# Hybrid conformer block on one core: the first head's far statistics by ScalarE's queue, and the output merges' first transfers earlier in the program

## The chip, the cores and the metric

The kernel runs on one core of one Trainium2 chip. The metric is the device time of one execution in microseconds (us). The core's engines are TensorE (PE, matmuls), VectorE (DVE), ScalarE (ACT), GpSimd (POOL) and SyncE (SP), which here only issues transfers (DMAs). Each engine runs its own instructions in order and waits for the others on semaphores. SyncE and ScalarE each have a queue on which they start DMAs; in the profile these appear as SPq and ACTq.

## What is computed

One block on 1024 tokens of width 1024, in float32: a norm, one wide projection, a gated depthwise convolution branch, an attention branch with 16 heads, a gated merge of the two, an output projection, and a gated feed-forward network. For this change the attention and the merge matter:

```python
DILATION_GROUPS = ((128, 1), (512, 4), (2048, 16))
...
    m = jnp.max(scores, axis=-1, keepdims=True)
    p = jnp.exp(scores - m)
    den = jnp.sum(p, axis=-1)
    o = jnp.einsum('nbhqk,nbkhd->nbqhd', p, vc) / jnp.swapaxes(den, 2, 3)[..., None]
    lse = jnp.swapaxes(m[..., 0] + jnp.log(den), 2, 3)
...
        mix = jax.nn.softmax(jnp.stack(lses), axis=0)
        o = jnp.einsum('gbsh,gbshd->bshd', mix, jnp.stack(outs))
        o = o.astype(x.dtype).reshape(B, S, ATTN_DIM)
        y_b = o @ w_attn_out[l].astype(o.dtype)

        g = jax.nn.sigmoid(gate_logits + gate_b[l].astype(gate_logits.dtype))
        g_a, g_b = jnp.split(g, 2, axis=-1)
        x = x + (g_a * y_a + g_b * y_b) @ w_out[l].astype(x.dtype)

        h = rms_norm(x, norm2_g[l])
```

Each query attends within three groups of keys (near ones, every fourth, every sixteenth), and the three softmaxes are mixed by the sums of their exponentials.

## The kernel before

**Products in three parts.** A float32 product is made of three TensorE passes: each operand is split into a high part (`hi`, rounded by ScalarE, L99) and a low part (`lo`, the rest, subtracted by VectorE, L100). The lines L131 to L133 are the three passes `hi*hi`, `hi*lo`, `lo*hi` of one step over 128 rows.

**The attention stage.** It is a loop over slots, eight for each of the 16 heads, four for each half of the queries. On ScalarE, VectorE, TensorE and GpSimd the order is written out by hand: it is the order in which the loop makes the instructions. SyncE's order is the scheduler's. In slot `at` the scores of the current unit are made (`score`, L1056 and L1057, the far group L1092), VectorE takes minima (`least`, L1060), and ScalarE takes exponentials with row sums (`powers`, L1101). Twelve slots later (`BACK = 12`) the unit is transposed by TensorE into a tile `pp` (`flip`, L1153), split into `ph` and `pl` (L1174, L1175), and two slots behind that multiplied with the values (`weigh`, L1191 and L1192). Between these, pieces of another matmul (the gate logits, later the convolution's output) fill TensorE (`fill`).

**The statistics.** For the second half of the queries a near part and a far part have minima and sums of their own, `own[h]`, in different layouts. Each part needs those of the other, `other[h]`. `near_to_far` sends the near part by four small transfers from SBUF to SBUF (L1118); `far_out` writes the far part to DRAM (`dstat`, L1121), and `far_to_near` reads it back in the other layout (L1125), five slots after the far scores (`READ = 5`). Then `compare` (L1129, L1130) and `combine` (L1135 to L1138) make the shares, and GpSimd multiplies the exponentials by them (`times`, L1104: four far products, then four near ones). The transposes of the far unit and of the second half wait for these. For the first head, whose far scores are made in slot 4, `far_to_near` stands in slot 9, `compare` in slot 13 and `combine` in slot 14; its far transposes stand in slot 16. For the other heads `compare` and `combine` stand one slot earlier each in relation to the head.

`tc.issue_after(x)` adds an edge of order behind `x` for what the block makes on the engine of `x`, and no wait across engines.

**The output merges.** When the heads are done, the attention output `do_` is read back from DRAM in pairs of rows (`o_fetch`: a raw part into a buffer `raw`, and a second part into the tile `oT`), added and split (`o_step`, L1228, L1224, L1221). Four `raw` buffers serve these and the weights (`stage`, L104; `wpiece`). Then `merge(c, w, half)` runs 16 times: three transfers (L1341 to L1343) bring two gate logits and the convolution branch into a tile `gg` (three buffers), ScalarE takes two sigmoids (L1346, L1347), VectorE multiplies (L1348), TensorE makes `yb` in one of four PSUM banks (24 matmuls), VectorE multiplies `yb` by its gate (L1355) and adds (L1356), and the sum is split into `mT` (L1358, L1359). The first four merges use the first half of the tokens, the next four the second half of the same weights. The row `gb2`, the second norm's factors spread over all partitions, is loaded ahead of the merges (L1336) and first read in the output projection (L1461).

Of the kernel before, what the change touches and what calls it, by code (L numbers as in the profile page):

```python
# [21 lines left out]
P = 128  # L22
# [47 lines left out]
def block_kernel(ctx: ExitStack, tc: tile.TileContext, x, xT, x0, g2, pack, mask,  # L70
# [957 lines left out]
    if True:  # L1028
# [94 lines left out]
        def far_to_near(h):  # L1123
            with tc.issue_after(queued[0].ins):
                sp.dma_start(other[h][:, 0], dstat[h % 2].rearrange("(i a) r s -> (a r) i s", i=4))  # L1125
# [83 lines left out]

        def o_fetch(half, k):  # L1210
            cs = slice(half * 512, half * 512 + 512)
            part = lambda i: do_[k : k + 2, i, :, cs].rearrange("k p t -> p k t")
            raw = stage(part(0), f"o_{half}{k}").rearrange("p (a b) -> p a b", a=2)
            hi, lo = (oT[i][half][:, k : k + 2, :] for i in range(2))
            fetch(lo, part(1))
            return raw, hi, lo
# [23 lines left out]
        with tc.manual_schedule(engines={ENG.Activation, ENG.DVE, ENG.PE, ENG.Pool}):  # L1240
# [3 lines left out]
            for at in range(len(slots) + BACK + 1):  # L1244
# [20 lines left out]
                for n, soon in enumerate(COPIES):  # L1265
                    if at == 0 and soon < 0 or cur is not None and (at - soon) % 8 == 0 and at - soon < len(slots):
                        by_residue((at - soon) // 8 if at else 0, n)
                flips = []
# [12 lines left out]
                for ago, ready in ((BACK - 3, combine), (BACK - 4, compare)):  # L1281
                    then = at - ago - (at < BACK + 4)
                    if 0 <= then < len(slots) and slots[then][1:] == (1, 0):
                        ready(slots[then][0])
# [16 lines left out]
                if at == len(slots) + BACK - 1:  # L1301
                    ao_first = [wpiece(w_ao[0], "ao0")]
# [22 lines left out]
    if True:  # L1325
        for a in range(2):
            oT[a].append(hb2_tile([P, KT, 512], F32R, f"hb{a}1", f"oT{a}1"))
        with tc.issue_after(settled_o[3].ins):
            ao_first += [wpiece(w_ao[c], f"ao{c}") for c in range(1, 4)]
        for k in range(0, KT, 2):  # L1330
            later = [o_fetch(1, k)]
            for _ in range(3):
                o_step(later)
        mT = hb_tiles(hb1, "mT")
        gb2 = p3.tile([P, D], F32, name="gb2")
        sp.dma_start(gb2, bass.AP(tensor=g2.tensor, offset=g2.offset, ap=[[0, P], [1, D]]))  # L1336
        def merge(c, w, half, between=None):
            cs = slice(half * 512, half * 512 + 512)
            gg = p3.tile([P, 3, 512], F32, tag="e", bufs=3, name=f"gg_{c}_{half}")
            ga, gb, ya = gg[:, 0], gg[:, 1], gg[:, 2]  # L1340
            sp.dma_start(ga, dgate[c][:, cs])  # L1341
            sp.dma_start(gb, dgate[8 + c][:, cs])
            sp.dma_start(ya, dya[c][:, cs])  # L1343
# [4 lines left out]
            dve.tensor_tensor(out=ya, in0=ya, in1=ga, op=ALU.mult)  # L1348
            yp = bank_ps(f"yb_{c}_{half}")
# [113 lines left out]

        for tt in range(8):
# [474 lines left out]
```

## Time and profile before

| What | us |
|---|---|
| three runs, median (lowest to highest) | 1667.54 (1666.99 to 1669.13) |
| the profiled execution | 1668.18 |
| its span in the trace | 1666.0 |
| TensorE busy | 1658.0 |
| VectorE busy | 1244.6 |
| ScalarE busy | 919.6 |
| GpSimd busy | 406.5 |

The granted TensorE clock was 1.00 throughout. Times in the trace are counted from the span's start. In a timeline row the first number is the start, the second the duration, both in us; then come engine, line of the kernel, operation, output<-input, partitions x elements, and how many instructions the row stands for. Brackets at the end give the idle time before the row and what ended it. In the view of waits the three numbers are the total in us, how often, and the longest. "DMA to landing" is the time from the issue of a transfer to its completion. Matmul durations are modelled and overlap, so the distance from start to start tells what one costs.

### The profile page before, as it was taken

The page shows a single profiled execution, that of the slowest core. Times are in us where ns is not written, and L with a number is a line of the kernel's source. Part 1 is how long each engine was busy: PE and PEld are TensorE (multiplying, and loading weights), DVE is VectorE, ACT ScalarE, POOL GpSimd, SP SyncE. Part 2 cuts the span into 40 slices and gives each one's busy share as a digit, 9 for nine tenths or more (in the row PEclk, how much of TensorE's full clock was granted, in tenths as well). Part 3 has the DMA queues.
Part 4 walks back from the last instruction along what each step waited for, and adds up shares of the span by engine and source line. Part 5 has one row for each costly group of instructions (what it writes and reads, how often), then busy time and mean ns, then how long its engine had stood idle before and what let it go on. Part 6 is the DMA issues. An engine that isn't in the chain of part 4 may idle for free.

```text
span 1666.0 us, 23008 instructions
## 1 busy us (share of the span) xinstructions
PE 1658.0 (100%) x7867; PEld 1384.3 (83%) x7867; DVE 1244.6 (75%) x1996; ACT 919.6 (55%) x1748; POOL 406.5 (24%) x450
## 2 busy tenths in 40 slices
PE   9999999999999999999999999999999999999999
PEld 7888888888888888888878888888888888888887
DVE  6999887879784568777567645878777777789863
ACT  5565555776665578777655434554444554544431
POOL 0023344877752355555310000000000000000000
PEclk9999999999999999999999999999999999999999
DMA  9111235344345879888587685422222222598851
GB/s 358 31 59 51 101 114 202 101 125 166 107 134 195 295 243 302 278 252 241 163 292 265 223 306 187 167 78 87 89 85 80 76 89 89 170 379 299 283 170 51
DMA packets 182341, 290.84 MB, mean 175 GB/s; under 512 B 31952, under 2 KB 89936, under 8 KB 181712
## 3 DMA queue, kind: packets, MB, share of 16 engines
q1 hardware_dynamic: 180928, 285.05, 51.2%
q10 hardware_dynamic: 1296, 4.33, 0.7%
q8 instruction: 62, 1.02, 0.2%
q14 instruction: 55, 0.45, 0.1%
HBM read 209.50 MB, written 79.76 MB: 174 GB/s over the span
## 4 chain that ended last, share of the span: by engine, by line
PE 96%; DMA 1%; DVE 1%; issue 1%; ACT 1%; POOL 0%; SPq 0%; POOLq 0%; DVEq 0%; ACTq 0%
PE dx L1745 7%; PE xz L156 6%; PE xz L158 6%; PE xz L157 6%; PE dy L1745 5%; PE qkv L150 5%; PE qkv L148 5%; PE qkv L149 5%; PE gx L158 3%; PE gx L156 3%; PE gx L157 3%; PE y L156 2%; PE y L158 2%; PE y L157 2%; PE pp L1153 2%; PE wo L150 2%
## 5 line engine op out<-in xcount | busy, mean ns | idle before, releaser
L572 POOL TENSOR_TENSOR codd<-codd,cpart 128x513 f32<-128x513 f32 x112 | 147.8, 1322 | 132.8 <-DVE lo_s L100 56.1
L148 PE MATMUL qkv<-qkv_hi,hT 128*128 128x512 f32 x384 | 152.7, 398 | 0.0
L150 PE MATMUL qkv<-qkv_hi,hT 128*128 128x512 f32 x384 | 150.3, 391 | 0.0
L149 PE MATMUL qkv<-qkv_lo,hT 128*128 128x512 f32 x384 | 149.9, 390 | 0.0
L1648 DVE SCALAR_TENSOR_TENSOR u<-u,pk 128x1023 f32<-128x1023 f32 x88 | 112.2, 1277 | 1.2 <-ACT u L1646 0.9
L621 DVE SCALAR_TENSOR_TENSOR conv<-csum,both,conv 128x512 f32<-128x512 f32 x120 | 90.2, 752 | 2.3 <-ACT conv L653 0.2
L621 DVE SCALAR_TENSOR_TENSOR conv<-apad,pk,conv 128x512 f32<-128x512 f32 x120 | 90.1, 751 | 1.6
L150 PEld LDWEIGHTS qkv<-qkv_hi,hT 128*128 128x128 f32 x384 | 72.1, 188 | 15.6
L149 PEld LDWEIGHTS qkv<-qkv_lo,hT 128*128 128x128 f32 x384 | 72.3, 188 | 14.6
L148 PEld LDWEIGHTS qkv<-qkv_hi,hT 128*128 128x128 f32 x384 | 72.2, 188 | 14.3
L100 DVE TENSOR_TENSOR lo_uv<-raw_uv,hi_uv 128x1024 fp32r<-128x1024 f32 x20 | 24.5, 1226 | 79.3 <-ACT hi_uv L99 79.3
L1175 DVE TENSOR_TENSOR pl<-pp,ph 128x512 fp32r<-128x512 f32 (+1 forms) x95 | 58.8, 619 | 30.4 <-ACT ph L1174 29.3
L586 ACT ACTIVATE cpart<-apad,pk 128x513 f32<-128x513 f32 x112 | 76.6, 744 | 2.1 <-POOL codd L572 2.0
L1060 DVE CUSTOM_DVE_ANT_0 p<-s,m 128x512 f32<-128x512 f32 (+1 forms) x120 | 59.1, 503 | 21.7 <-POOL p L1104 16.2
L156 PE MATMUL xz<-h2left,hi_uv 128*128 128x512 f32 x176 | 68.6, 390 | 0.0
L156 PE MATMUL xz<-blk_t,hi_s3g 128*128 128x512 f32 x176 | 68.5, 389 | 0.0
L158 PE MATMUL xz<-h2left,lo_uv 128*128 128x512 f32 x176 | 68.5, 389 | 0.0
L158 PE MATMUL xz<-blk_t,lo_s3g 128*128 128x512 f32 x176 | 68.5, 389 | 0.0
L157 PE MATMUL xz<-h2left,hi_uv 128*128 128x512 f32 x176 | 68.5, 389 | 0.0
L157 PE MATMUL xz<-blk_t,hi_s3g 128*128 128x512 f32 x176 | 68.5, 389 | 0.0
L1174 ACT ACTIVATE ph<-pp 128x512 fp32r<-128x512 f32 (+1 forms) x95 | 51.2, 539 | 28.4 <-PE pp L1153 27.6
L124 POOL TENSOR_TENSOR rs<-ss,mhalf 128x8 f32<-128x8 f32 x32 | 53.6, 1677 | 36.3 <-DVE ss L123 34.2
(479 smaller groups left out, 5185.2 us busy)
## 6 DMA issues: line engine op xcount, KB each, us to landing
wr<-w_down SPq DMA_DIRECT2D x45, 512.0 KB, 6.1
kk<-dk SPq DMA_DIRECT2D x32, 512.0 KB, 6.1
gr<-dff SPq DMA_DIRECT2D x62, 256.0 KB, 5.6
raw_qkv<-w_qkv SPq DMA_DIRECT2D x24, 512.0 KB, 4.6
raw_g<-w_ch SPq DMA_DIRECT2D x23, 512.0 KB, 3.7
dff<-u SPq DMA_DIRECT2D x22, 512.0 KB, 2.6
raw_uv<-w_up SPq DMA_DIRECT2D x21, 512.0 KB, 3.6
raw_ug<-w_up SPq DMA_DIRECT2D x20, 512.0 KB, 3.7
```

Source lines behind the costliest of these rows:

```text
L148: pe.matmul(ps, ah, hi[:, k % 2, :], start=(k == 0), stop=False)
L149: pe.matmul(ps, ah, lo[:, k % 2, :], start=False, stop=False)
L150: end = pe.matmul(ps, al, hi[:, k % 2, :], start=False, stop=(k == KT - 1))
L156: pe.matmul(o, wh[:, k, :], bh[:, k, :], start=(start and k == 0), stop=False, skip_group_check=not start)
L157: pe.matmul(o, wh[:, k, :], bl[:, k, :], start=False, stop=False, skip_group_check=not start)
L158: end = pe.matmul(o, wl[:, k, :], bh[:, k, :], start=False, stop=(k == 3), skip_group_check=not start)
L572: r = pool.tensor_tensor(out=out, in0=in0, in1=in1, op=op)
L586: act.activation(part, zo[:, i : i + 513], AF.Copy, scale=taps[:, c, 2 * i + 1 : 2 * i + 2])
L621: dve.scalar_tensor_tensor(out=out_, in0=src[:, i : i + 512], scalar=w, in1=out_, op0=ALU.mult, op1=ALU.add)
L1060: dve.tensor_tensor_reduce(out=pt, in0=s, in1=m, scale=-1.0, scalar=3e38, op0=ALU.add, op1=ALU.min, accum_out=nm)
L1648: dve.scalar_tensor_tensor(out=acc[:, d:], in0=src[:, : T - d], scalar=w(2 - d), in1=acc[:, d:], op0=ALU.mult, op1=ALU.add)
L1745: pe.matmul(banks[n][:, cols], a[:, c], b[:, d], start=(start and i == 0 and m == 0), stop=(stop and i == nf - 1 and m == 2), skip_group_c ...
```

## The change

Two places are changed.

In the attention stage the first head's `far_to_near` is issued by ScalarE instead of SyncE. The first head's `compare` stays in slot 13 but stands ahead of that slot's `flip`, and its `combine` moves from slot 14 to slot 13, behind `weigh` and `result`. The other heads keep their slots.

Ahead of the merges the raw parts of the first two pairs of the second half (`o_raw`) and the second weight piece (`ao1`) are loaded in the loop's last slot but one, in the order ao0, ao1, o part 0, o part 2. The transfers, sigmoids and first product of the first merge (`gate_pair(0, 0)`) stand ahead of the last `o_fetch`. The `gb2` row is loaded behind the last merge's transfers.

```diff
         def far_to_near(h):
             with tc.issue_after(queued[0].ins):
-                sp.dma_start(other[h][:, 0], dstat[h % 2].rearrange("(i a) r s -> (a r) i s", i=4))
+                (sp if h else act).dma_start(other[h][:, 0], dstat[h % 2].rearrange("(i a) r s -> (a r) i s", i=4))
...
+        o_raws = {}
+
+        def o_part(half, k, i):
+            return do_[k : k + 2, i, :, half * 512 : half * 512 + 512].rearrange("k p t -> p k t")
+
+        def o_raw(half, k):
+            return stage(o_part(half, k, 0), f"o_{half}{k}").rearrange("p (a b) -> p a b", a=2)
+
         def o_fetch(half, k):
-            cs = slice(half * 512, half * 512 + 512)
-            part = lambda i: do_[k : k + 2, i, :, cs].rearrange("k p t -> p k t")
-            raw = stage(part(0), f"o_{half}{k}").rearrange("p (a b) -> p a b", a=2)
+            raw = o_raws.pop((half, k)) if (half, k) in o_raws else o_raw(half, k)
             hi, lo = (oT[i][half][:, k : k + 2, :] for i in range(2))
-            fetch(lo, part(1))
+            fetch(lo, o_part(half, k, 1))
             return raw, hi, lo
...
+                if at == BACK + 1:
+                    compare(0)
                 flips = []
...
                 for ago, ready in ((BACK - 3, combine), (BACK - 4, compare)):
-                    then = at - ago - (at < BACK + 4)
-                    if 0 <= then < len(slots) and slots[then][1:] == (1, 0):
-                        ready(slots[then][0])
+                    if BACK <= at - ago < len(slots) and slots[at - ago][1:] == (1, 0):
+                        ready(slots[at - ago][0])
+                if at == BACK + 1:
+                    combine(0)
...
                 if at == len(slots) + BACK - 1:
-                    ao_first = [wpiece(w_ao[0], "ao0")]
+                    ao_raws = [stage(w_ao[c], f"ao{c}") for c in range(2)]
+                    for k in (0, 2):
+                        o_raws[1, k] = o_raw(1, k)
+                    ao_first = [wpiece(w_ao[0], "ao0", ao_raws[0])]
...
         with tc.issue_after(settled_o[3].ins):
-            ao_first += [wpiece(w_ao[c], f"ao{c}") for c in range(1, 4)]
+            ao_first += [wpiece(w_ao[c], f"ao{c}", ao_raws[1] if c == 1 else None) for c in range(1, 4)]
+        gated = {}
+
+        def gate_pair(c, half):
+            cs = slice(half * 512, half * 512 + 512)
+            gg = p3.tile([P, 3, 512], F32, tag="e", bufs=3, name=f"gg_{c}_{half}")
+            ga, gb, ya = gated[c, half] = gg[:, 0], gg[:, 1], gg[:, 2]
+            sp.dma_start(ga, dgate[c][:, cs])
+            sp.dma_start(gb, dgate[8 + c][:, cs])
+            gated["last"] = sp.dma_start(ya, dya[c][:, cs])
+
+            with tc.issue_after((read_out[H - 1, 1] if c or half else highs[-2]).ins):
+                act.activation(ga, ga, AF.Sigmoid, bias=pk[:, C_GB + c : C_GB + c + 1])
+                act.activation(gb, gb, AF.Sigmoid, bias=pk[:, C_GB + 8 + c : C_GB + 9 + c])
+            dve.tensor_tensor(out=ya, in0=ya, in1=ga, op=ALU.mult)
+
         for k in range(0, KT, 2):
+            if k == KT - 2:
+                gate_pair(0, 0)
             later = [o_fetch(1, k)]
...
-        gb2 = p3.tile([P, D], F32, name="gb2")
-        sp.dma_start(gb2, bass.AP(tensor=g2.tensor, offset=g2.offset, ap=[[0, P], [1, D]]))
...
         def merge(c, w, half, between=None):
...
+            if (c, half) not in gated:
+                gate_pair(c, half)
+            ga, gb, ya = gated.pop((c, half))
             yp = bank_ps(f"yb_{c}_{half}")
...
+        gb2 = p3.tile([P, D], F32, name="gb2")
+        with tc.issue_after(gated["last"].ins):
+            sp.dma_start(gb2, bass.AP(tensor=g2.tensor, offset=g2.offset, ap=[[0, P], [1, D]]))
         for tt in range(8):
             x2, ps = wo_tile(0, tt, wo_first)
```

More of the change, by code (lines that the diff above doesn't have):

```diff
@@ L1334, in block_kernel @@
         mT = hb_tiles(hb1, "mT")
-        gb2 = p3.tile([P, D], F32, name="gb2")
-        sp.dma_start(gb2, bass.AP(tensor=g2.tensor, offset=g2.offset, ap=[[0, P], [1, D]]))
         def merge(c, w, half, between=None):
[L1338 to L1343, printed above, removed]
-            with tc.issue_after((read_out[H - 1, 1] if c or half else highs[-2]).ins):
-                act.activation(ga, ga, AF.Sigmoid, bias=pk[:, C_GB + c : C_GB + c + 1])
-                act.activation(gb, gb, AF.Sigmoid, bias=pk[:, C_GB + 8 + c : C_GB + 9 + c])
-            dve.tensor_tensor(out=ya, in0=ya, in1=ga, op=ALU.mult)
+            if (c, half) not in gated:
+                gate_pair(c, half)
+            ga, gb, ya = gated.pop((c, half))
             yp = bank_ps(f"yb_{c}_{half}")
```

## The prediction

> **What bounds the kernel now.** I read the page's chain first, then the waits of TensorE, then the two places that they name.
>
> ```profile
> PE 96%; DMA 1%; DVE 1%; issue 1%; ACT 1%; POOL 0%; SPq 0%; POOLq 0%; DVEq 0%; ACTq 0%
> ```
>
> TensorE is the bound: 96% of the chain that ended last is matmuls, which the change does not touch. So the change can only take away time in which TensorE stands still. The view of TensorE's waits lists all of that which it can name:
>
> ```profile
> PE yb L131 <- DVE gg L1355: 1.2, 1, 1.2
> PE glu L446 <- ACT whi_gv L436: 1.1, 1, 1.1
> PE early L489 <- POOL ones L365: 1.0, 1, 1.0
> PE pp_far L1153 <- POOL pf_first L1104: 0.7, 1, 0.7
> PE o L1192 <- DVE pl L1175: 0.2, 1, 0.2
> ```
>
> Two of five rows lie where the change works: pp_far (the first head's far transposes) and yb (the output merges). The glu and early rows belong to the first stage, ahead of every edited line. A wait in this view is only the clean gap; a group that is fed piece by piece is stretched too. So I price both places by start-to-start times. First head, timeline of TensorE:
>
> ```profile
> 584.65 0.42 PE L1056 MATMUL s<-kk,q 128*128 128x384 f32 x1
> ...
> 589.60 0.50 PE L1056 MATMUL s<-kk,q 128*128 128x512 f32 x1
> ...
> 592.66 0.39 PE L1056 MATMUL s<-kk,q 128*128 128x384 f32 x1
> ...
> 595.31 0.28 PE L1056 MATMUL s<-kk,q 128*128 128x256 f32 x1
> ```
>
> The same four score matmuls one head later, with the same work between them:
>
> ```profile
> 603.32 0.39 PE L1056 MATMUL s<-kk,q 128*128 128x384 f32 x1
> ...
> 608.11 0.40 PE L1056 MATMUL s<-kk,q 128*128 128x512 f32 x1
> ...
> 608.58 0.60 PE L1153 MATMUL pp_far<-ident,pf 128*128 128x128 f32 x4
> ...
> 609.42 0.39 PE L1056 MATMUL s<-kk,q 128*128 128x384 f32 x1
> ...
> 611.66 0.28 PE L1056 MATMUL s<-kk,q 128*128 128x256 f32 x1
> ```
>
> Stretch by stretch the first head is longer by 4.95 - 4.79 = 0.16, 3.06 - 1.31 = 1.75 and 2.65 - 2.24 = 0.41: **2.32 us** lost, three times what the wait row shows. Second place, the merges:
>
> ```profile
> 850.98 0.39 PE L131 MATMUL yb<-oT,hi_ao 128*128 128x512 f32 x1
> ...
> 872.52 0.39 PE L133 MATMUL yb<-oT,lo_ao 128*128 128x512 f32 x1
> 874.06 0.50 PE L131 MATMUL yb<-oT,hi_ao 128*128 128x512 f32 x1 [1.15 <-DVE gg L1355]
> ```
>
> Four merges run in 21.54 us, 95 steps of 0.227. The step to the fifth takes 1.54: 1.54 - 0.23 = **1.31 us** lost. All that the change can win here is 2.32 + 1.31 = 3.6 us, 0.22% of the run.
>
> **The first head's statistics.** The chain that ends in the stall, engine by engine:
>
> ```profile
> 590.62 1.41 POOL L1104 TENSOR_SCALAR pf_first<-pf_first,both 128x128 f32<-128x128 f32 x4 [6.11 <-DVE both L1138]
> ```
> ```profile
> 588.71 0.17 DVE L1129 TENSOR_TENSOR both<-own,other 128x8 f32<-128x8 f32 x1 [2.69 <-DMA dstat<-own]
> ```
> ```profile
> 576.26 0.45 SPq L1121 DMA_DIRECT2D dstat<-own  x1
> ...
> 579.47 1.21 SPq L1118 DMA_DIRECT2D other<-own  x2
> ...
> 582.68 0.44 SPq L1125 DMA_DIRECT2D other<-dstat  x1
> ```
> ```profile
> other<-own SPq DMA_DIRECT2D x8, 1.0 KB, 4.7
> dstat<-own SPq DMA_DIRECT2D x2, 4.0 KB, 4.1
> ```
> ```profile
> L1125 SPq DMA_DIRECT2D other<-dstat x1: 436/436/436, 582.7 to 582.7; - x1
> ...
> DMA to landing us min/median/max: 5.8/5.8/5.8
> ```
>
> GpSimd multiplies late because VectorE's compare waited until 588.71. The wait is put down to a dstat transfer, but the data that compare needs is the return (L1125): issued at 582.68, landed at 582.68 + 5.8 = 588.5. What it reads was written at 576.26 + 4.1 = 580.4, and the other sums (L1118) landed at about 580.1 + 4.7 = 584.8. So the return sat some 2 us in SyncE's queue with nothing to wait for but its place there.
>
> The edit puts this one return on ScalarE's queue, behind the exponentials of slot 9. The order edge to the mask load is one of SyncE's order, so it falls away. ScalarE then stands at the issue until the write has landed, and the rows of its program there are:
>
> ```profile
> 580.33 0.19 ACT L1101 ACTIVATION_READ_ACCUMULATOR p<-p,st 128x1 f32 x1
> ...
> 582.28 0.40 ACT L1101 ACTIVATE p<-p,st 128x128 f32<-128x128 f32 x1 [0.75 <-DVE st L1060]
> ```
> ```profile
> L713 ACTq DMA_DIRECT2D da<-apad x7: 326/326/327, 535.9 to 551.2; - x7
> ...
> DMA to landing us min/median/max: 2.6/2.7/4.4
> ```
>
> The issue costs 0.33 (ScalarE's own rows) to 0.44 (this transfer on SyncE), after a wait of 0 to 0.2. Queued behind it are the split hi_gt, two exponentials and the first head's first ph; 0.75 us of idle before 582.28 swallows all of it. I count nothing. If that cover were gone, ph would be half a microsecond late, for a product that TensorE runs two slots later.
>
> The transfer leaves at 580.6 and lands between 580.6 + 2.6 = 583.2 (ScalarE queue's fastest row) and 580.6 + 5.8 = 586.4 (its own row). I take the slow end, since this is the same transfer in the same load. Compare then starts at 586.6 instead of 588.71. From compare to GpSimd the trace takes 590.62 - 588.71 = 1.91, with one 0.55 score reduction and one 0.55 pl between the small operations; in one slot only the pl is left between, so 1.4 to 1.9. GpSimd starts at 588.0 to 588.5, and its four far products end 1.41 later, at 589.4 to 589.9. TensorE wants the first at about 589.9 (in the next head pp_far lies 608.58 - 608.11 = 0.47 behind its score; 589.60 - 0.16 + 0.47). The 1.75 goes. The 0.16 goes with it, since it was the score reduction of slot 14 queued behind the late compare. Of the 0.41, what GpSimd's four further products leave late: they end about 2.15 after the far ones, near 591.6 to 592.0, and TensorE is there at about 591.8. I leave 0.2 as a residual, between 0 (landing at 583) and 0.9 (landing at 587). Saved: 2.32 - 0.2 = 2.1. What is queued behind the waiting compare on VectorE is the pl of slot 13, which TensorE multiplies in slot 15, at 588.6; with compare over by 587.0 it is in time.
>
> Beside that sum stands a rule. The Trainium skill ("DMA: Bandwidth & Descriptors", Issuing engines are not separate DMA queues) says that issuing from several engines saves only the sequencer's issue time, as all share the same 16 DMA engines. By it the transfer still takes 5.8, which is the end that I took; the 2.7 of ScalarE's rows speaks for less, but those ran in another stage, and with it the residual would be 0.
>
> The changed loop condition gives heads 1 to 15 the slots they had, and the first head's own are written out; no cost.
>
> **The merges.** The rows of the fifth merge's wait:
>
> ```profile
> 870.65 1.28 ACT L1346 ACT_TABLE_LOAD   x1
> ```
> ```profile
> 873.31 0.69 DVE L1355 TENSOR_TENSOR gg<-yb,gg 128x512 f32<-128x512 f32 x1
> ```
> ```profile
> L1343 SPq DMA_DIRECT2D gg<-dya x1: 320/320/320, 863.1 to 863.1; - x1
> ...
> DMA to landing us min/median/max: 9.0/9.0/9.0
> ```
>
> and of the view by stretches the one from 868 to 872 (its last two numbers are the DMA engines' busy share and GB/s):
>
> ```profile
> 868.00:872.00 4.00, 4.00 (x19) 3.34 (x18) 3.58 (x3) 3.40 (x4) 0.00 (x0) 1.00 1.05 390
> ```
>
> The fifth merge wants the first merge's bank, free when L1355 ends at 874.0. That waited for the sigmoid, a 1.28 table load, the last o half's split ahead of it on ScalarE, and transfers that took 9.0 to land (until 872.1), queued behind 512 KB of g2 row and the last o parts. The DMA engines are full there: at 390 GB/s a transfer of 512 KB takes 1.34. After the change the three gate transfers go out before the last o pair, the g2 row is gone from ahead of them, and two raw o parts were fetched before the rush. So five such transfers fall away from ahead of the gates, 6.7 us; the third raw o part, which finds its buffer later, gives back 2 to 3. I expect the gates 4 to 7 us earlier, in place by 865 to 868, the sigmoids and the table load at 866 to 869, and L1355 behind the last o's additions at 868 to 872. TensorE wants the bank at 872.75, so all 1.31 is gone if L1355, 0.69 long, starts by 872.0; by what it starts later, the 1.31 shrinks, down to nothing. I take it whole. Next late is the last o pair: TensorE reads it six of eight k steps, 6 x 0.68 = 4 us, into the fifth merge, near 876.8, and VectorE had settled it before L1355 at 873.3; it may come 3 us later and cost nothing.
>
> The early raw parts take two of four raw buffers, so ao2 and ao3 load later; that is the slower rival below. The g2 row moves behind the last merge's transfers; VectorE first reads it at 993.79, some 50 us after, so it costs nothing:
>
> ```profile
> 993.79 1.28 DVE L1461 SCALAR_TENSOR_TENSOR x<-x,s,gb 128x1024 f32<-128x1024 f32 x1 [0.74 <-POOL s L124]
> ```
>
> **Sum.** 2.1 + 1.3 = 3.4 us. The profiled execution took 1668.18 (its span of 1666.0 and 2.2 around it), so 1664.8; it lies 0.64 above the median of the three runs, 1667.54, from which I get **1664.1**. Behind both places TensorE has no waits left to take the gain back, so it should reach the end whole.
>
> **Rivals.**
> - *The return lands no sooner* (0.12): held on ScalarE by an older transfer, or slow, it lands at 588.5 again. Compare, earlier in the program, then holds pl back as well; only about 0.5 is won from the shorter chain. 0.5 + 1.3 gives 1665.7. Against it: the 2 us of pure queueing above.
> - *The merges' gates come no sooner* (0.12): the last o pair, whose raw buffers come free later now, holds L1355 to 874. 2.1 alone gives 1665.4.
> - *Neither works* (0.08): 1667.5. This includes that the stalls move to the next thing late.
> - *Slower: ao2's buffer* (0.08). ao2 and ao3 are now the fifth and sixth to ask for a buffer, not the third and fourth; ao2 gets that of the first half's last o part, or has to wait for an early raw part's.
>
> ```profile
> 851.49 1.22 DVE L1221 TENSOR_TENSOR oT<-raw_o,oT 128x1024 fp32r<-128x1024 f32 x1
> ```
> ```profile
> 852.74 0.38 SPq L104 DMA_DIRECT2D raw_o<-do  x1
> ```
> ```profile
> raw_qkv<-w_qkv SPq DMA_DIRECT2D x24, 512.0 KB, 4.6
> ```
>
> A raw buffer goes to the next load as soon as it is free (851.49 + 1.22 = 852.71, load at 852.74). If ao2 gets that one, it lands at 857.3 and is split by 859.8; the third merge starts at 850.98 + 2 x 5.44 = 861.9, so all is well. If it must wait for an early raw part to be settled (about 863), it lands at 867.6 and is split a microsecond later: TensorE stands 6.8 us. With the bank wait hidden in it that is 1667.5 - 2.1 - 1.3 + 6.8 = 1670.9. It decides from a load later than about 856.
>
> **How the numbers follow.** The forecast has 0.60, with its own range of 1663.3 to 1664.9 (residual 0 to 0.9, and a few tenths for the runs' spread). The range of 1662.8 to 1666.2 holds it and the first two rivals, 0.84, with a little lost at the edges. A measurement of this kernel tells about 0.2% from no change, which is 1664.2 here: 0.7 of the forecast's case lies below it, since its residual is as likely 0 as 0.4, and the runs lie as much below as above. Faster 0.42; same 0.18 + 0.24 + 0.08 = 0.50; slower 0.08.
>
> **What would show it.** Right: no pp_far and no yb row in TensorE's waits; the first head's stretches of 4.8, 1.3 and 2.2 us like the second head's; GpSimd's first far product less than 4.5 us behind TensorE's score of slot 14; ScalarE's return landed by 587; the table load before 869. Wrong: a wait on hi_ao or lo_ao in the third merge, a TensorE wait on ph_first or pl in slots 14 to 16, or a new wait anywhere behind 880, where the shifted g2 row and transfers lie.

## The result and the profile after

| | before | after |
|---|---|---|
| median of 13 runs each, us | 1668.54 | 1665.6 |
| lowest to highest | 1665.57 to 1670.44 | 1663.56 to 1666.71 |
| profiled execution | 1668.18 | 1664.8 |
| its span | 1666.0 | 1662.7 |

The ratio after to before is 0.9982 with an interval of 0.9973 to 0.9990: 2.9 us won, between 1.7 and 4.5.

The view of TensorE's waits of the changed kernel (engine, line, tile <- what ended the wait: total us, times, longest):

```profile
PE early L489 <- POOL ones L365: 1.0, 1, 1.0
PE o L1192 <- DVE pl L1175: 0.2, 1, 0.2
PE s L1056 <- DMA kk<-dk: 0.2, 1, 0.2
```

Both rows that the change worked on, pp_far and yb, are gone. So is the glu row of the first stage; it lies ahead of any edit, so this is scatter of the start. The first head, timeline of TensorE (start, duration):

```profile
583.95 0.42 PE L1056 MATMUL s<-kk,q 128*128 128x384 f32 x1
...
588.77 0.40 PE L1056 MATMUL s<-kk,q 128*128 128x512 f32 x1
...
589.24 0.68 PE L1153 MATMUL pp_far<-ident,pf_first 128*128 128x128 f32 x4
...
590.16 0.39 PE L1056 MATMUL s<-kk,q 128*128 128x384 f32 x1
...
591.28 1.00 PE L1153 MATMUL pp<-ident,p_first 128*128 128x128 f32 x4
...
592.82 0.27 PE L1056 MATMUL s<-kk,q 128*128 128x256 f32 x1
```

The stretches from score to score are 4.82, 1.39 and 2.66. Against the second head of the kernel before (4.79, 1.31, 2.24) they lose 0.03 + 0.08 + 0.42 = 0.53; before, it was 2.32. What feeds them, from the return of the statistics (line L1125, its transfer and landing) over VectorE to GpSimd:

```profile
L1125 ACTq DMA_DIRECT2D other<-dstat x1: 403/403/403, 578.9 to 578.9; - x1
...
DMA to landing us min/median/max: 7.6/7.6/7.6
```
```profile
586.67 0.17 DVE L1129 TENSOR_TENSOR both<-own,other 128x8 f32<-128x8 f32 x1 [2.06 <-DMA dstat<-own]
```
```profile
588.11 1.42 POOL L1104 TENSOR_SCALAR pf_first<-pf_first,both 128x128 f32<-128x128 f32 x4 [4.29 <-DVE both L1138]
589.50 2.18 POOL L1104 TENSOR_SCALAR p_first<-p_first,both 128x512 f32<-128x512 f32 x4
```

The return lands at 578.9 + 7.6 = 586.5, compare starts at 586.67, GpSimd at 588.11. Its last near product ends at 589.50 + 2.18 = 591.68, and the pp row that wants it began at 591.28 and is stretched to 1.00: that is the 0.42.

The merges, timelines of ScalarE, VectorE and TensorE:

```profile
864.73 1.28 ACT L1353 ACT_TABLE_LOAD   x1
```
```profile
867.40 0.69 DVE L1375 TENSOR_TENSOR gg<-yb,gg 128x512 f32<-128x512 f32 x1
```
```profile
870.49 0.39 PE L133 MATMUL yb<-oT,lo_ao 128*128 128x512 f32 x1
870.72 0.39 PE L131 MATMUL yb<-oT,hi_ao 128*128 128x512 f32 x1
```

The fifth merge's first matmul (870.72) stands 0.23 behind the fourth's last: no wait. Bank and gates are ready 2.6 us early (867.40 + 0.69 = 868.09).

**Where the time went.** The distance of one head's far scores (s_far, L1092) to the next head's is 16.355 when nothing waits, so two make 32.71; from the second head's to the third's, where the first head's statistics fall, the shortest seen in any run is 15.40. Four such rows of the changed kernel, of heads 1, 2, 5 and 7, counted from 0:

```profile
580.84 0.74 PE L1092 MATMUL s_far<-far_k,far_q 128*128 128x256 f32 x4
596.76 0.64 PE L1092 MATMUL s_far<-far_k,far_q 128*128 128x256 f32 x4
...
645.82 0.64 PE L1092 MATMUL s_far<-far_k,far_q 128*128 128x256 f32 x4
...
679.11 0.64 PE L1092 MATMUL s_far<-far_k,far_q 128*128 128x256 f32 x4
```

The first head loses 596.76 - 580.84 - 15.40 = 0.52, and heads 5 and 6 together lose 679.11 - 645.82 - 32.71 = 0.58. With the steps between the yb matmuls beyond 0.23, the main losses of every kernel of this study can be read this way, one trace of each. "Start" is the first s_far row, behind which all edits lie; "return lands" is the landing of the first head's return (L1125), counted from the start and good to a tenth; "ao1" is the loss in the first merge, at the second weight piece; "bank" is the loss at the fifth merge; "rest" is the span less the start and the four losses.

| kernel | start | return lands | first head | heads 5, 6 | ao1 | bank | span | rest |
|---|---|---|---|---|---|---|---|---|
| before | 570.99 | 17.5 | 2.32 | 0.12 | 0 | 1.42 | 1666.0 | 1091.15 |
| after | 570.29 | 16.2 | 0.52 | 0.58 | 0 | 0 | 1662.7 | 1091.31 |
| e1 head only | 570.33 | 13.5 | 0.00 | 2.31 | 0.58 | 0.79 | 1665.1 | 1091.09 |
| e2 merges only | 569.86 | 16.4 | 1.29 | 0.14 | 1.27 | 0 | 1663.7 | 1091.14 |
| e3 return by SyncE | 570.61 | 18.0 | 2.37 | 1.43 | 0 | 0 | 1665.5 | 1091.09 |
| e4 old slots | 570.15 | 17.1 | 1.97 | 0.59 | 0.91 | 0 | 1664.6 | 1090.98 |
| e5 gates only | 570.52 | 14.4 | 0.03 | 1.17 | 0 | 0 | 1662.8 | 1091.08 |
| e6 raw parts only | 570.72 | 17.6 | 1.91 | 0.97 | 0 | 0 | 1664.7 | 1091.10 |
| e7 row only | 570.40 | 13.7 | 0.04 | 0.36 | 0.44 | 1.04 | 1663.6 | 1091.32 |
| e8 last by VectorE | 570.58 | 17.2 | 1.20 | 0.80 | 1.17 | 0 | 1664.8 | 1091.05 |
| e9 merge order | 570.47 | 15.4 | 0.04 | 0.58 | 0.29 | 0 | 1662.5 | 1091.12 |
| e10 head, early a | 570.77 | 15.9 | 0.23 | 0.00 | 0.88 | 0.84 | 1663.9 | 1091.18 |
| e11 all three | 570.52 | 16.0 | 0.03 | 0.00 | 0.29 | 0 | 1662.3 | 1091.46 |

The rest is the same within 0.5 us in thirteen kernels, so these few places hold nearly all that differs. The bank column has the step of 1.31 and one of 0.11 right behind it, the ao1 column likewise. Between before and after the profiled spans differ by 3.3: the start 0.70 (no edit), the first head 1.80, the merges 1.42, given back at heads 5 and 6 0.46, rest 0.16.

### The profile page after: what moved, and what is told of

Same layout as the page of the kernel before. It is cut to its first block, busy times and chain, and to the rows that moved or that the text cites. A ratio compares the mean times of both kernels' runs of the same rounds, so it can differ in the third digit from the quotient of the medians.

```text
span 1662.7 us, 23007 instructions
## 1 busy us (share of the span) xinstructions
PE 1657.5 (100%) x7867; PEld 1384.9 (83%) x7867; DVE 1243.3 (75%) x1996; ACT 919.6 (55%) x1748; POOL 406.8 (24%) x450
## 4 chain that ended last, share of the span: by engine, by line
PE 96%; DMA 1%; DVE 1%; issue 1%; ACT 0%; POOL 0%; SPq 0%; POOLq 0%; ACTq 0%
PE dx L1768 7%; PE xz L156 6%; PE xz L158 6%; PE xz L157 6%; PE dy L1768 5%; PE qkv L150 5%; PE qkv L148 5%; PE qkv L149 5%; PE gx L158 3%; PE gx L157 3%; PE gx L156 3%; PE y L156 2%; PE y L158 2%; PE y L157 2%; PE pp L1153 2%; PE wo L149 2%
## 5 line engine op out<-in xcount | busy, mean ns | idle before, releaser
L150 PEld LDWEIGHTS qkv<-qkv_hi,hT 128*128 128x128 f32 x384 | 72.1, 188 | 15.7
```

The lines of the kernel that those rows point to most:

```text
L150: end = pe.matmul(ps, al, hi[:, k % 2, :], start=False, stop=(k == KT - 1))
```

## The experiments

### One place alone: e1 and e2

e1 takes the head's edits and leaves the merges as they were; e2 the other way round. The diff of e1 is the change's own first half:

```diff
-                sp.dma_start(other[h][:, 0], dstat[h % 2].rearrange("(i a) r s -> (a r) i s", i=4))
+                (sp if h else act).dma_start(other[h][:, 0], dstat[h % 2].rearrange("(i a) r s -> (a r) i s", i=4))
...
+                if at == BACK + 1:
+                    compare(0)
...
+                if at == BACK + 1:
+                    combine(0)
```

> The kernel before with the first head's two edits alone (return on ScalarE's queue, compare and combine both in slot 13). Theory: in the trace of the change the four start-to-start stretches of the first head lost 0.42 + 0.08 + 0.03 us against the next head where the kernel before lost 2.32, so 1.8 us come from here: about 1666.7 against 1668.5, and TensorE's waits keep the yb row of 1.2 us and lose the pp_far row. Rival: the first head's gain was scatter of one execution (its dstat write went out 1.8 us earlier against TensorE than in the trace of before, ahead of any edited instruction); then the compare starts no earlier against TensorE than before and the stretches stay longer by 1.5 us or more.

> The kernel before with the merges' edits alone (raw parts and ao1 ahead, first gates ahead, g2 row behind). Theory: 1.3 us, all of it at the fifth merge, so about 1667.2 against 1668.5; the yb row leaves TensorE's waits, the pp_far row of 0.7 stays and the first head's stretches stay longer by some 2.3 us. Rival: the two places are not independent (the merges' transfers were in time only because the attention stage ended 2 us earlier in relation to them): then a yb wait of some tenths stays.

e1: ratio to before 0.9989 (0.9980 to 0.9998). e2: 0.9991 (0.9982 to 0.9999). Added, -1.1 and -0.9 per mille make -2.0, where both together measured -1.8: no part spoils the other by an amount that these runs can tell. By the ratios e1 won 1.8 us (0.3 to 3.3) and e2 1.5 (0.2 to 3.0), so the times can't tell either from the loss of its place in the table. But in the traces each gave something back elsewhere. Waits of TensorE, e1:

```profile
PE ya L131 <- DVE pl L1175: 0.9, 1, 0.9
PE yb L131 <- DVE gg L1358: 0.5, 1, 0.5
PE yb L131 <- ACT hi_ao L99: 0.3, 1, 0.3
```

The first head is clean to the last tenth, and then 2.31 us go at heads 5 and 6, where the kernel before lost 0.12. Timeline of ScalarE there, and of VectorE behind it:

```profile
650.96 0.63 ACT L204 ACTIVATE aT<-raw_a 128x512 fp32r<-128x512 f32 x1 [1.26 <-DMA raw_a<-da]
```
```profile
652.00 0.56 DVE L1175 TENSOR_TENSOR pl<-pp,ph 128x384 fp32r<-128x384 f32 x1 [1.26 <-ACT ph L1174]
...
667.72 0.17 DVE L1129 TENSOR_TENSOR both<-own,other 128x8 f32<-128x8 f32 x1 [0.71 <-DMA vf<-dv]
```

A split for the convolution's output, in ScalarE's hand-written order, waits 1.26 us for a load raw_a; ph, pl and the combine of head 5 stand behind it, its far transposes come late, and a head later a compare waits too and holds the pl for which ya waits. The DMA engines are full ahead of it. The stretch from 630 to 650 of the changed kernel, with the DMA engines' busy share and GB/s at the end:

```profile
630.00:650.00 20.00, 20.00 (x126) 17.73 (x125) 15.93 (x60) 16.35 (x49) 10.13 (x16) 1.00 0.96 291
```

The share is 0.96 at 291 GB/s here, 0.94 in e1 and 0.97 in the kernel before, which lost only 0.12; so a full stretch by itself does not make the loss. What goes with it is the wait of this split: 1.26 in e1, 0.13 to 0.93 in the other eight kernels with the head's edits, whole or in part, and the old requests for raw_a, none in the kernel before and in e2. The lead of TensorE is not the whole cause either: e3 below, which gained nothing in the first head (2.37), waited 0.84 for the same load and lost 1.43.

e2 has no bank wait, but another in the first merge:

```profile
849.05 0.39 PE L132 MATMUL yb<-oT,hi_ao 128*128 128x512 f32 x1
850.45 0.50 PE L131 MATMUL yb<-oT,hi_ao 128*128 128x512 f32 x1 [1.01 <-ACT hi_ao L99]
```

The scheduler, which orders the merges, puts two matmuls of the second merge ahead of the first merge's third, so a late second weight piece (ao1) holds TensorE at 850.45: 1.27 us, of which the kernel before and the changed one lost nothing.

e2's first head lost 1.29 where some 2.3 was expected, though none of its code differs from the kernel before: its return landed 16.4 behind the start, not 17.5. So about 1 us of such a loss is scatter of one run, and the 1.80 between the two traces above is not all the edit's. The seven kernels with all of the head's edits and no others there lost 0.40 in the mean, the two with none 1.8; that difference of 1.4 and e1's 1.8 are the better measures.

### One half of the head's edits: e3 and e4

e3 is the changed kernel with the return on SyncE again; e4 with compare and combine in their old slots.

```diff
-                (sp if h else act).dma_start(other[h][:, 0], dstat[h % 2].rearrange("(i a) r s -> (a r) i s", i=4))
+                sp.dma_start(other[h][:, 0], dstat[h % 2].rearrange("(i a) r s -> (a r) i s", i=4))
```
```diff
-                if at == BACK + 1:
-                    compare(0)
...
-                    if BACK <= at - ago < len(slots) and slots[at - ago][1:] == (1, 0):
-                        ready(slots[at - ago][0])
-                if at == BACK + 1:
-                    combine(0)
+                    then = at - ago - (at < BACK + 4)
+                    if 0 <= then < len(slots) and slots[then][1:] == (1, 0):
+                        ready(slots[then][0])
```

> The changed kernel with the first head's return on SyncE's queue again; compare and combine stay together in slot 13. Theory (the queue carries the gain): the return goes out some 2 to 3 us later against TensorE and lands 1 to 1.3 us later, GpSimd's far products start about 589 on the clock of the trace of the change instead of 588.1, and the first head's stretches are longer than the next head's by 1.3 to 1.8 us instead of 0.5; a TensorE wait on pp_far of some 0.3 us or a wait on pl in slot 15 appears. Rival (the slots carry it): they stay at 0.5 to 0.8.

> The changed kernel with compare and combine at their old places in slots 13 and 14; the return stays on ScalarE's queue. Theory (the queue carries most, the slots about 0.5): compare starts at the same time, GpSimd's far products some 0.4 us later than in the trace of the change, and the first head's stretches are longer than the next head's by about 0.9 to 1.1 us instead of 0.5. Rival (the slots carry it): 1.5 or more, with the pp_far wait back at 0.5 or more.

One run each: 1667.54 and 1666.58. e3, timeline of VectorE and waits of TensorE:

```profile
588.83 0.17 DVE L1129 TENSOR_TENSOR both<-own,other 128x8 f32<-128x8 f32 x1 [3.96 <-DMA dstat<-own]
```
```profile
PE o L1192 <- DVE pl L1175: 1.6, 2, 1.4
```

The stall stays whole (2.37) and only moves: compare, now earlier in VectorE's order, waits 3.96 us and holds the pl of slot 13, for which TensorE waits 1.4. e4, with compare at its old place:

```profile
587.50 0.17 DVE L1129 TENSOR_TENSOR both<-own,other 128x8 f32<-128x8 f32 x1 [1.93 <-DMA dstat<-own]
```
```profile
589.42 0.72 POOL L1104 TENSOR_SCALAR pf_first<-pf_first,both 128x128 f32<-128x128 f32 x2 [5.32 <-DVE both L1138]
```

Compare to GpSimd takes 1.92, as before; 588.11 - 586.67 = 1.44 in the changed kernel. Both expectations missed: e3 lost 2.37, not 1.3 to 1.8, and e4 1.97, not 0.9 to 1.1. In one trace each, neither half alone took the stall away. But their returns also landed 1.8 and 0.9 later behind the start than the changed kernel's, and part of that is scatter, so these two runs alone do not tell what a half is worth.

The table tells more. With both edits the loss follows the landing: 0.00 to 0.04 where it lands 13.5 to 15.4 us behind the start, 0.23 at 15.9, 0.52 at 16.2, 1.20 at 17.2 (e8, helped by its own edit), 1.91 at 17.6 (of the last two, 0.28 and 0.75 have another cause, which comes with e6). With the old slots it is 1.29 at 16.4, 1.97 at 17.1 and 2.32 at 17.5: some 0.6 to 1.2 more for about the same landing. That is what the slots are worth, read from few points. The other gain is the queue. In all ten kernels with the return on ScalarE it left 0.07 to 0.08 us behind the landing of the dstat write that it reads. On SyncE it left 2.13 (before), 1.57 (e2) and 1.75 (e3) behind it. In the kernel before the write landed at 580.55, and SyncE issued three other transfers before the return at 582.68:

```profile
580.73 0.59 SPq L167 DMA_DIRECT2D kk<-dk  x1
581.37 0.58 SPq L980 DMA_DIRECT2D m<-mask  x1
582.05 0.38 SPq L247 DMA_DIRECT2D dgate<-gs  x1
```

So the return landed at 13.5 to 17.6 on ScalarE's queue, 15.7 in the mean of ten kernels, and at 16.4, 17.5 and 18.0 on SyncE's, 17.3 in the mean of three.

### One of the merges' three edits: e5, e6, e7

Each has the head's edits and one of: the gate transfers ahead of the last pair (e5), two raw parts and ao1's raw part ahead (e6), the gb2 row behind (e7). As an example, e5 against the changed kernel:

```diff
-                    ao_raws = [stage(w_ao[c], f"ao{c}") for c in range(2)]
-                    for k in (0, 2):
-                        o_raws[1, k] = o_raw(1, k)
-                    ao_first = [wpiece(w_ao[0], "ao0", ao_raws[0])]
+                    ao_first = [wpiece(w_ao[0], "ao0")]
...
-            ao_first += [wpiece(w_ao[c], f"ao{c}", ao_raws[1] if c == 1 else None) for c in range(1, 4)]
+            ao_first += [wpiece(w_ao[c], f"ao{c}") for c in range(1, 4)]
...
+        gb2 = p3.tile([P, D], F32, name="gb2")
+        sp.dma_start(gb2, bass.AP(tensor=g2.tensor, offset=g2.offset, ap=[[0, P], [1, D]]))
...
-        gb2 = p3.tile([P, D], F32, name="gb2")
-        with tc.issue_after(gated["last"].ins):
-            sp.dma_start(gb2, bass.AP(tensor=g2.tensor, offset=g2.offset, ap=[[0, P], [1, D]]))
```

> The changed kernel's head edits, and of the three merge edits only one: the gate transfers ahead of the last pair of o parts. Raw o parts are fetched as in the kernel before, the g2 row stands before the first merge. Theory: the place of the gates is what counts, since SyncE's queue works in order: the table load stands before 869 less the shift of the start, and the step to the fifth merge loses 0 (bound 0.3). Rival, the one of the prediction's sum: five transfers had to fall away from ahead of the gates, of which the last pair is only two and the g2 row one more that now stands behind; then 0.3 to 0.8 of the 1.31 stays. Time: 1664.3 to 1666 for one look, span 1662.5 to 1664, by what heads 5 and 6 (0.1 to 2.3) and ao1 (0 to 1.2) lose.

> The changed kernel's head edits, and of the three merge edits only one: two raw o parts and ao1's raw part ahead. Gate transfers and the g2 row stand where they did. Theory: SyncE reaches the gates no earlier than the last pair's buffer comes free, so the step to the fifth merge still loses 0.5 to 1.3, as in the head-only kernel (0.68) and the kernel before (1.31). Rival: the early parts take the rush away and the step loses under 0.3. Apart from it: ao1's raw part asked for earlier makes the wait on hi_ao1 0 by the rule that the changed kernel's zero comes from it; if that wait is 0.3 or more here, the early ask isn't what makes it.

> The changed kernel's head edits, and of the three merge edits only one: the g2 row, 512 KB, behind the last merge's transfers; gates and raw parts stand where they did. Theory: one transfer of 1.34 us less ahead of the gates; the step to the fifth merge loses 0 to 0.7, some 0.7 to 1.3 less than before's 1.31 when the lead of the head is counted in. Rival: SyncE waits at the last pair's buffer, and the row goes out in that wait or behind it for nothing: the loss is that of the head-only kernel, 0.7 to 1.3. In no case does the row's late place cost anything behind 880: the stretch from the fifth merge's first step to the end is as long as in the kernel before, within 0.15.

One run each: 1664.69, 1666.81, 1665.38. The table load on ScalarE, in this order of kernels:

```profile
864.17 1.28 ACT L1350 ACT_TABLE_LOAD   x1 [0.88 <-DMA gg<-dgate]
```
```profile
867.90 1.28 ACT L1353 ACT_TABLE_LOAD   x1 [1.32 <-DMA gg<-dgate]
```
```profile
866.64 1.28 ACT L1350 ACT_TABLE_LOAD   x1 [0.29 <-DMA gg<-dgate]
```

Counted from each kernel's first yb matmul (849.25, 851.21, 848.36) that is 14.9, 16.7 and 18.3; 19.7 in the kernel before, and 15.8 with all three (864.73 - 848.93). The bank loss: 0, 0 and 1.04. The gates alone are enough, as the theory had it. The raw parts alone are enough too, where my theory expected 0.5 to 1.3 and the rival was right; that the rush is shorter without the two parts is the likely reason, not one that a run isolates. The row alone wins nothing, as its rival had it: e1 and e10, with none of the three, lost 0.79 and 0.84. All seven kernels with the three together lost nothing there. Its late place costs nothing either: e7's fifth merge starts at 871.52 and the end comes 792.08 later, in the kernel before 1666.0 - 874.06 = 791.94.

Asking for ao1 early is not what spares its wait: e2, e4 and e8 ask early and lost 0.91 to 1.27 there, while e5 and the kernel before do not and lost nothing.

e6 lost 1.91 in the first head, though its code there is the changed kernel's. Part of it is a price that I had put at nothing. Timeline of ScalarE in e6 and in e8 (below), then of TensorE in e6:

```profile
581.77 0.64 ACT L204 ACTIVATE hi_gt<-raw_gt 128x512 fp32r<-128x512 f32 x1 [1.51 <-DMA dstat<-own]
```
```profile
581.18 0.63 ACT L204 ACTIVATE hi_gt<-raw_gt 128x512 fp32r<-128x512 f32 x1 [1.05 <-DMA dstat<-own]
```
```profile
585.12 0.41 PE L1056 MATMUL s<-kk,q 128*128 128x384 f32 x1 [0.50 <-DVE st L1107]
```

ScalarE stands at the issue until the write of dstat has landed, here 1.51 and 1.05 us, and by the score of slot 14 TensorE is 0.75 and 0.28 late, against e5, where ScalarE stood for 0.67 and TensorE lost nothing. The cover of 0.75 that the prediction found holds to a tenth; the waits are longer than the 0 to 0.2 that it allowed.

### What the changed kernel still lost: e8 to e11

e8 gives the last of the first head's near products to VectorE. e9 adds an order edge that keeps the second merge behind the first. e10 is e1 with the loads raw_a asked one gate earlier. e11 is the changed kernel with all three.

```diff
-            for i in (7, 6, 4, 5):
+            for i in (7, 6, 4, 5) if h else (7, 6, 4):
...
+                if at == BACK + 3:
+                    p5 = pts[0, 5][0]
+                    dve.tensor_scalar(p5, p5, first_shares[0][:, 0, 1:2], 1.0, op0=ALU.mult, op1=ALU.mult)
```
```diff
-            for _ in gemm_half(yp, w, oT, half):
-                pass
+            with tc.issue_after(yb_end[0].ins) if (c, half) == (1, 0) else ExitStack():
+                for _ in gemm_half(yp, w, oT, half):
+                    pass
+            yb_end[:] = gemm_end
```
```diff
-                    each = KT // len(seconds)
-                    for k in range(seconds.index(c) * each, (seconds.index(c) + 1) * each, 2):
+                    for k in ((0, 2), (4,), (6,), ())[seconds.index(c)]:
```

> The changed kernel, but the last of the first head's four near products (sub-tile 5) is multiplied by VectorE at the end of slot 15 and not by GpSimd. Theory: the 0.43 us that the first head's third stretch still loses (2.66 against 2.23) is GpSimd's line of eight products, the last of which ends at 591.7, behind the time at which TensorE wants it; with seven on GpSimd the third stretch falls to 2.2 to 2.35 and the three stretches' loss from 0.54 to 0.1 to 0.25; span 0.3 to 0.45 shorter, if nothing later takes it. Rival: the loss is set by when compare ends (586.84), or by DMA traffic of those microseconds; then the third stretch stays at 2.6 to 2.7. Second rival: VectorE's product in slot 15 delays the pl of that slot, and a TensorE wait on pl of 0.2 to 0.5 appears in its place.

> The changed kernel, but with an order edge that puts all matmuls of the second output merge behind those of the first. Theory: the waits of 0.47 to 1.17 us on hi_ao1 that the head-only, merges-only and old-slots kernels showed come from the planned order alone, which puts two matmuls of the second merge ahead of the first merge's last; with the edge, TensorE reads ao1 only 5.4 us after the first merge's start, and no wait on hi_ao or lo_ao shows anywhere; the time is the changed kernel's, 1664 to 1665.5 for one look, with the span's 0 to 0.2 either way, as its own trace lost nothing there. Rival: the landing of ao1 is late for the first merge as well, and a wait of 0.3 or more stays between the first and the second merge.

> The head edits alone, with the gated convolution's reads of the rows a asked one gate earlier (two at the first gate, one at the second, one at the third, none at the fourth; before, one at each). Theory: the 2.31 us that the head-only kernel lost at heads 5 and 6 are ScalarE's transposed split of raw_a, held by a transfer that is asked for too late in a stretch in which the DMA engines are full; asked for earlier, the two intervals of heads 5 and 6 sum to 32.7 to 32.9 (loss 0 to 0.2, against 2.31 head only and 0.58 changed), ScalarE's wait ahead of that split names no DMA; the fifth merge's bank wait of 0.7 to 1.3 stays. Rival: the DMA engines are full, so that an earlier read only makes another one late: the loss stays above 0.4, or a wait of the same size appears on q, kk or the gate in heads 4 to 7.

> The changed kernel with all three additions: the last near product on VectorE, the second merge behind the first, the rows a one gate earlier. Theory: the losses that the changed kernel still has are 0.54 in the first head, 0.58 at heads 5 and 6, and none to about 1 at ao1, by the run; of these 0.3 to 0.45, 0.4 to 0.58 and 0 to 0.5 are won: 0.7 to 1.5 below the changed kernel, a ratio to the kernel before of 0.9972 to 0.9980 and a span of 1661.2 to 1662.2 in the profile. Rival: the stretch with full DMA engines takes back what the first head wins, as it did for the head-only kernel; then the span stays at 1662.4 to 1663 and the ratio at 0.998 to 0.9985.

**e8**, one run, 1666.63. The third stretch, timeline of TensorE, and the product on VectorE:

```profile
591.45 0.39 PE L1056 MATMUL s<-kk,q 128*128 128x384 f32 x1
...
593.78 0.28 PE L1056 MATMUL s<-kk,q 128*128 128x256 f32 x1
```
```profile
590.86 0.77 DVE L1299 TENSOR_SCALAR p_first<-p_first,both 128x256 f32<-128x256 f32 x1
```

593.78 - 591.45 = 2.33, where the changed kernel had 2.66: the theory holds for this stretch. But this run's return landed 1.0 later than the changed kernel's, the two stretches ahead lost 0.81, and ScalarE's wait cost the 0.28 told above. So the first head lost 1.20, not the 0.1 to 0.25 expected. The total says nothing of the edit; the stretch does.

**e9**, one run, 1664.56: the expectation missed in part. TensorE's weight loads in the first merge, and ScalarE's split of ao1:

```profile
849.27 0.19 PEld L135 LDWEIGHTS yb<-oT,lo_ao 128*128 128x128 f32 x1 [0.45 <-DVE lo_ao L100]
```
```profile
848.70 1.06 ACT L99 ACTIVATE hi_ao<-raw_ao 128x1024 fp32r<-128x1024 f32 x1 [0.74 <-DMA raw_ao<-w_ao]
```

ao1 was late again (0.74) and did not matter. But now the first merge's own lo_ao is waited for, 0.29 us, which the two matmuls that the scheduler puts there had covered. e11 shows the same 0.29. The edge trades a loss of 0 to 1.27, by the run, for a certain 0.29.

**e10**, one run, 1665.7. The split of raw_a has no wait, and heads 5 to 7 run without a loss (678.74 - 646.03 = 32.71):

```profile
642.93 1.16 ACT L204 ACTIVATE aT<-raw_a 128x512 fp32r<-128x512 f32 x2
```
```profile
646.03 0.64 PE L1091 MATMUL s_far<-far_k,far_q 128*128 128x256 f32 x4
...
678.74 0.64 PE L1091 MATMUL s_far<-far_k,far_q 128*128 128x256 f32 x4
```

Loss 0.00 here and in e11, against 0.36 to 2.31 in the nine kernels that have the head edits, whole or in part, and the old requests. The theory holds; the rival of full DMA engines does not, since their share from 630 to 650 is 1.00 in e10. The bank's 0.84 stayed, as expected; a wait of 0.3 in the first stage (psr) lies ahead of the edits.

**e11**: median 1664.35 (11 runs, 1663.41 to 1664.91), before beside it 1667.68; ratio 0.9977 (0.9968 to 0.9986). The ratio came as the theory had it; the span of 1662.3 lies between the theory's 1661.2 to 1662.2 and the rival's 1662.4 to 1663. First head 0.03 with the return landing at 16.0, where 0.2 to 0.5 would be due without the product on VectorE. Beside the 0.29 at lo_ao, which stands in the weight loads, TensorE's waits are two, neither of them touched by the change or the additions:

```profile
PE early L490 <- POOL ones L366: 1.0, 1, 1.0
PE o L1196 <- DVE pl L1179: 0.2, 1, 0.2
```

That is 3.3 us less than before by the medians. The interval overlaps the changed kernel's, and the two were not timed side by side, so that e11 is the faster is likely by the table but not shown.

## Why the prediction was right, point by point

- **TensorE is the bound and only its stalls can be won**: right. The rest column is the same with all edits and with none.
- **The return leaves earlier, lands in its own 5.8, compare at 586.6, GpSimd at 588.0 to 588.5**: right in place, by two errors that cancel. It left at 578.9, not 580.6, and took 7.6, not 5.8; compare started at 586.67, GpSimd at 588.11. That it left earlier than foreseen comes from ahead of the edit: the dstat write itself was issued 3.46 behind the start, in the kernel before 5.27. The queueing was the loss: from issue to landing the return took 4.1 to 7.6 on ScalarE's queue in ten kernels, on SyncE's 5.7, 5.8 and 6.6, with means of 6.1 and 6.0. This agrees with the Trainium skill ("DMA: Bandwidth & Descriptors", Issuing engines are not separate DMA queues): the queue does not make the transfer faster. What the Trainium skill calls usually small there, the time saved on the sequencer, was the gain here: the three issues ahead of the return and the gaps between them made 2.13 between the write's landing and the return's issue, and on ScalarE's 0.08 is left of it.
- **The issue costs nothing on ScalarE, after a wait of 0 to 0.2, under a cover of 0.75**: true in the changed kernel's trace (rows in the last section). But the wait was mis-sized: in ten kernels ScalarE stood at the issue for 0 to 1.51, and beyond 0.75 the rest went to TensorE.
- **Residual of the first head 0.2, between 0 and 0.9**: 0.52 in this trace, and of the kind named, GpSimd's near products; e8 shows it by taking one away. In seven kernels with the same first-head code (after, e1, e5, e6, e7, e9, e10) it was 0.00 to 1.91, four times under 0.05. My upper end of 0.9 was too low: it allowed a landing at 587, 16.0 behind the start, and e6's came at 17.6.
- **The 1.31 of the merges goes whole**: right (1.42 with a small gap behind it). The gates landed at 856.3 + 8.4 = 864.7, before at 872.1; the table load at 864.73 was expected at 866 to 869, L1375 at 867.40 at 868 to 872. My account of why was partly off. In the kernel before the table load followed with 0.02 idle on ScalarE's split of the last o half (869.57, 1.06 long), and the first gate had landed just before, at 870.11; so the place in ScalarE's order and the transfers were late together, and `gate_pair` moves both. Five transfers fewer ahead was more than was needed: e5 and e6 show that moving the gates, or fetching the raw parts early, suffices alone.
- **The last o pair may come 3 us later**: it was settled at 878.4, before at 871.9, 6.5 later, past the 876.8 at which I had TensorE read it. It cost nothing because the scheduler has TensorE take steps of the next merges ahead of the fifth's last ones: no merge ends before 882.28, 11.6 behind the fifth's first matmul, where a merge by itself takes 5.4. The outcome was right, the cover was not the one that I named.
- **Slower, by ao2's buffer**: did not happen. The loads went out well before the 856 from which it would decide, the row of SyncE's queue:

```profile
851.01 1.55 SPq L104 DMA_DIRECT2D raw_ao<-w_ao  x2
```

- **"Behind both places TensorE has no waits left to take the gain back"**: this step failed. The list of waits of one trace shows only what was late in that trace. Heads 5 and 6 stood close behind their loads without a row in the list; against the kernel before they took back 0.46 in this trace and 2.19 in e1, and e10 shows that it was the loads. And ao1, for which neither the kernel before nor the changed one waits, cost 0.4 to 1.3 in six of the nine others without e9's edge.
- **The sum**: 3.4 was forecast, 2.9 measured (1.7 to 4.5). In the traces the two places gave 1.80 + 1.42 = 3.22, and heads 5 and 6 took back 0.46. The step from the profiled time to the median was off as well: I took 0.64 off because the profile lay above the median of three runs, but of 13 runs the median is 1668.54, above the profile. So the forecast of 1664.1 is 1.5 below the 1665.6 that came: 1.0 from that, 0.5 from the gain. 1665.6 lies outside the forecast's own 1663.3 to 1664.9 and inside the wide range of 1662.8 to 1666.2, close to the times of the first two rivals (1665.7 and 1665.4), whose mechanisms did not come. That the wide range held is in part luck too. That the profiled execution took the very 1664.8 of the sum is luck as well: 0.70 of its lead was there ahead of the first edit.

## What to carry to other kernels

A list of waits names what is late, not what is nearly late: before a gain is carried to the end, look in every stretch with full DMA engines behind it for loads that land just in time, and ask for them earlier in the same edit. A wait that is moved up in an engine's order holds what stands behind it, so move it together with the data that it waits for (in e3 the wait alone moved the stall to a pl). Split a span into its start and the few intervals that can stretch; then one trace says to tenths of a microsecond where that run's time went, which the medians of a dozen runs do not. What an edit is worth still takes several traces: the same code lost 0.00 to 1.91 in the first head.

## What the runs showed of the hardware

ScalarE's sequencer issued the transfer ahead of an exponential that stands before it in its program. Timeline of ScalarE and its queue in the changed kernel:

```profile
578.64 0.58 ACT L246 ACTIVATE gs<-gate 128x512 f32<-128x512 f32 x1
578.89 0.40 ACTq L1125 DMA_DIRECT2D other<-dstat  x1
579.12 0.61 ACT L1101 ACTIVATE p<-p,st 128x384 f32<-128x384 f32 x1
```

In the program the order is gs, the 128x384 exponential, the transfer. The issue lies at 578.89 within gs's 0.58, and the exponential follows 0.48 behind gs, without idle time: here the sequencer ran ahead of the engine, and the issue cost the engine's work nothing. Where the write landed later, the issue held the engine: the split hi_gt behind it stood idle for 0.23 to 0.41 in e11, e1 and e10, up to the length of the issue itself (0.38 to 0.40), and longer where the write landed later still, up to 1.51 in e6.

The same small transfer took 4.1 to 7.6 us in ten kernels with the same code up to it, and the write ahead of it landed 8.5 to 10.5 behind the start. With them the first head's loss goes from 0.00 to 1.91 us in kernels with the same code there, more than most edits here win.
